# Channel mixers of a two-layer encoder: a tile's convolution tap and its adding transfer stand behind the next tile's weight sums and weights' adding transfer

## The chip, the cores and the metric

One core of a Trainium2 chip runs the whole program in one launch. The metric is the device time of that launch in microseconds (us). Engines are named as in the profile: PE (matrix products), DVE (VectorE), ACT (ScalarE), POOL (GpSimd) and SP (SyncE); SP and POOL also issue DMA transfers.

## What is computed

The program is a trunk of two layers over 512 tokens of width 1024: a layer with an RWKV-7 time mixer, and one with chunked attention; each also attends to 256 memory tokens, and each ends in a channel mixer. Only the channel mixers matter here:

```python
def conv_glu(h, w_in, conv_w, conv_b, w_out):
    seq = h.shape[1]
    gate, val = jnp.split(h @ w_in, 2, axis=-1)
    gp = jnp.pad(gate, ((0, 0), (CONV_W - 1, 0), (0, 0)))
    conv = conv_b + sum(conv_w[j] * gp[:, j:j + seq] for j in range(CONV_W))
    return (jax.nn.gelu(conv, approximate=False) * val) @ w_out

# in each layer
x = x + conv_glu(rms_norm(x, ln2[layer]), ffn_in[layer], ffn_conv[layer],
                 ffn_conv_b[layer], ffn_out[layer])
```

All is float32. The hidden width is 2816, which is 22 tiles of 128 channels; the convolution has three taps along the tokens.

## The kernel before

Every float32 product is made of three products of a faster type: an operand is split into a high part (ACT casts it) and a low part (what the cast left, by a subtraction on DVE or by a transfer that adds), and high x high, high x low and low x high are summed in PSUM.

`ffn` computes a channel mixer with the hidden channels on the partitions and the 512 tokens along the free dimension. Tiles 0 to 20 of the 22 are objects of the class `Seven`: instead of eight half-size products a tile takes seven, by sums and differences of blocks (a Strassen-like scheme). For that each tile needs sums of its weight blocks. A tile's raw weights lie in a buffer `raw` of seven 128x512 blocks: G1, V1, G2, V2 are loaded (`load`, on SP's queue, two tiles ahead), and the rest are sums:

- `sums` (L515) makes S3 and S1 in one operation on DVE, `sum2` (L520) makes S2 from S1, `sum4` (L524) makes S4 from S2.
- `rest` (L499, L500) makes the low part of G2 and V2: ACT writes the negated high part into `wlv`, and a transfer on POOL's queue adds the raw weights from DRAM to it.
- `high` (L528) casts two blocks on ACT: G1 with S2, then S3 with S1, then G2 with V2, then S4. `lower` (L533) subtracts on DVE.
- Nine tiles of the 21 (even numbers 2 to 18, `apart`) make the low part of G1 by a transfer too (`rest1`, L505 and L506); for them DVE makes only the low part of S2 (`both`, L510). The others make both in one wider L533. So tiles alternate between two kinds.

The end of a tile runs while the next two are multiplied: `end1` (L539) and `endr` (L542) finish the gate `g` and scale it by the norm, `end2` (L555) starts `c` on ACT with the third tap and the bias, `end3` (L559) adds the second tap on DVE, `endt` (L545) scales the first tap on ACT into a spare block (in r1h, r1l, r2h or r2l), and `endd` (L552) adds that block to `c`, two tokens later, by a transfer on POOL's queue. One tile later `end4` (L562) is the Gelu on ACT and `end5` (L566) the product with the value half, on DVE.

`frame` writes one tile's work out by hand, in this order around the change: the product of the gate weights, the casts of G2 and S4, the low parts of S3 and S4, the `end1`, `endr`, `end2` and `endt` of the tile before (`prev`), the difference L603, then the changed place, then `end4` and `end5` of the tile before that (`prev2`), L616, and the low part of the next tile's G1 and S2. `keep` pins the instructions of ACT and DVE in the order written; each engine runs its own in order. The transfers of POOL's queue are not pinned, but each stands in its queue in order too. L500 and L506 fill weights of the next tile (`nxt`); PE uses L500's late in that tile, as L465.

The edited lines run where a tile has one before and one behind it: tiles 1 to 19, in two mixers, 38 times in all.

Of the kernel before, what the change touches and what calls it, by code (L numbers as in the profile page):

```python
# [90 lines left out]
def halved(t):  # L91
    return t.rearrange("p (a b) -> p a b", a=2)


def plain_order(ps):
    return ps.rearrange("p (b a) -> p a b", a=2)
# [37 lines left out]
def trunk_kernel(ctx, tc, A, out):  # L134
# [52 lines left out]
    def ps_f():  # L187
        return banks["F"].tile([P, S], F32, name="psf", tag="psf")
# [8 lines left out]
    def tmp(dt=F32, shape=(P, S)):  # L197
        return banks["tmp"].tile(list(shape), dt, name="tmp", tag="tmp")
# [67 lines left out]
    def run(g):  # L266
        for y in g:
            assert not callable(y) or y()
# [166 lines left out]
    def ffn(l, hp, U, T, new_x, xT, after=None, tokens=None):  # L435
# [10 lines left out]
        def prod(ps, w, x, late=False):  # L446
            (wh, wl), o, *ol = w
            ol = ol[0] if ol else o
            for ks in ((0, 1, 2), (3,)) if late else (range(4),):
                for k in ks:  # L450
                    for n in range(2):
                        PE.matmul(ps, wh[:, o + k * P:o + k * P + P], x[k][n], start=k == n == 0, stop=False)  # L452
                for k in ks:
                    PE.matmul(ps, wl[:, ol + k * P:ol + k * P + P], x[k][0], start=False, stop=k == 3)  # L454

        def high_part(ps, w, x):
            (wh, _), o = w
            for k in range(4):
                for n in range(2):
                    PE.matmul(ps, wh[:, o + k * P:o + k * P + P], x[k][n], start=k == n == 0, stop=False)  # L460

        def low_part(ps, w, x):
            (_, wl), o = w
            for k in range(4):
                PE.matmul(ps, wl[:, o + k * P:o + k * P + P], x[k][0], start=False, stop=k == 3)  # L465
# [3 lines left out]
        def keep(ins):  # L469
            return tc.keep_in_program_order(ins) if pinned[0] else ins  # L470
# [5 lines left out]
        class Seven:  # L476
# [91 lines left out]
            def frame(self, prev2, prev, nxt, norm=None, ending=None):  # L568
                first = prev is None
                if first:  # L570
                    nxt.load()
                f1, f2, f3, self.f4 = (ps_f() for _ in range(4))
                g = self.g = tmp()
                prod(f1[:, h1], (self.gs, 0), XU(0, 0))
                if first:
                    hv = self.hv
                    turns["whi"] = (turns["whi"] + 1) % 3
                    self.h31 = self.high(S3)
                    turns["whi"] = (turns["whi"] + 1) % 3
                else:  # L580
                    hv = self.high(G2)
                keep(SC.copy(halved(g[:, h1]), plain_order(f1[:, h1])))
                if nxt and nxt.apart:
                    nxt.rest1()
                if first:
                    prod(self.f4[:, h1], ((hv, self.lows[0]), 0), XU(1, 0), True)
                if norm and not first:
                    run(norm)
                w31 = self.lower(S3, self.h31)
                if prev:  # L590
                    prev.end1()
                    prev.endr()
                prod(f2[:, h1], (self.gs, S), XT(T2), first)
                w4 = self.lower(S4, self.high(S4, S), S)
                if self.j + 2 < NFF - 1:
                    made[self.j + 2].load()
                if nxt and prev:
                    prev.end2()
                    prev.endt()
                elif prev:  # L600
                    next(ending)
                    next(ending)
                keep(V.tensor_tensor(halved(g[:, h2]), halved(g[:, h1]), plain_order(f2[:, h1]), op=ALU.subtract))  # L603
                if nxt and prev:
                    prev.end3()
                    prev.endd()
                if nxt:
                    nxt.sums()
                    nxt.sum2()
                    nxt.rest()  # L610
                if nxt and prev2:
                    prev2.end4()
                    prev2.end5()
                c = self.c = tmp()
                prod(f1[:, h2], (w31, 0), XT(T3))
                keep(V.tensor_tensor(halved(c[:, h1]), plain_order(f1[:, h2]), halved(g[:, h2]), op=ALU.subtract))  # L616
                if first:
                    next(norm)
                prod(f3[:, h2], (w31, S), XT(T1))
                if nxt:  # L620
                    if nxt.apart:
                        nxt.both()
                    else:
                        nxt.gs = nxt.lower(G1, nxt.high(G1))
                    nxt.sum4()
                else:
                    next(ending)
                if first:
                    next(norm)
                v = self.v = tmp()  # L630
                if first:
                    prod(f3[:, h1], ((hv, self.lows[1]), S, 0), XT(T4))
                else:
                    both = ((f3[:, h1], ((hv, self.low), S), XT(T4)), (self.f4[:, h1], ((hv, self.low), 0), XU(1, 0)))
                    for p in both:
                        high_part(*p)
                    low_part(*both[0])
                keep(V.tensor_tensor(v[:].rearrange("p (h a b) -> p h a b", h=2, a=2), halved(c[:, h1]).unsqueeze(1).to_broadcast([P, 2, 2, P]),  # L638
                                     f3[:].rearrange("p (h b a) -> p h a b", h=2, a=2), op=ALU.add))
                keep(V.tensor_tensor(halved(g[:, h2]), halved(g[:, h2]), plain_order(f3[:, h2]), op=ALU.subtract))  # L640
                if nxt:
                    nxt.h31 = nxt.high(S3)
                else:
                    next(ending)
                if not first:
                    low_part(*both[1])
                prod(self.f4[:, h2], (w4, 0), XU(1, 1))
# [1427 lines left out]
```

## Time and profile before

| | us |
|---|---|
| three runs | 1267.63, 1269.70, 1272.45 |
| their median | 1269.7 |
| the profiled execution | 1270.51 |
| its span, first to last instruction | 1268.7 |
| busy: PE, weight loads (PEld), DVE, ACT, POOL | 1229.1, 1078.4, 1032.1, 839.8, 151.1 |
| the first mixer's tiles | about 392 to 592 |
| the second mixer's tiles | about 940 to 1140 |

The granted clock was 0.996 over the span. A row of the timeline gives start, duration, engine, source line, operation, the names out<-in, the shapes and how often; in brackets stands how long the engine had been idle before and who ended that. In a row of waits stand the total, the number and the longest, in us. "DMA to landing" is the time from issue to the last byte's signal, min, median and max.

### The profile page before, as it was taken

Reading aid. Unit: us, or ns where it says so; the run is one execution under the profiler, and the core shown is the slowest. Engines: PE = TensorE matmul, PEld = TensorE weight load, DVE = VectorE, ACT = ScalarE, POOL = GpSimd, SP = SyncE. Lnnn points to the kernel's source line nnn. Section 1 sums busy time; section 2 is a strip of 40 time slices with the busy share of each in tenths; the row PEclk is TensorE's granted clock in tenths of the full one; section 3 lists DMA queues with packets and bytes.
Section 4 is the critical chain, followed back from the end, with each engine's and each line's share of the span. In section 5 each row is a group of like instructions: output and inputs, shape, how many; then the busy total and the mean of one; then the engine's idle time right before and its main releaser. Section 6 shows DMA issues by size and latency. Waiting matters only on the chain.

```text
span 1268.7 us, 26433 instructions
## 1 busy us (share of the span) xinstructions
PE 1229.1 (97%) x10420; PEld 1078.4 (85%) x10420; DVE 1032.1 (81%) x1958; ACT 839.8 (66%) x1396; POOL 151.1 (12%) x180
## 2 busy tenths in 40 slices
PE   9999999999999999999999999999999999999997
PEld 6787777777788999999888878777789999998886
DVE  7976677766678999999886976658889999999785
ACT  6557668766566777776564676767767777765672
POOL 1000000000001222221120000000002322211200
PEclk9999999999999999999999999999999999999999
DMA  6355454353064989985994332233428989878961
GB/s 207 101 166 125 89 114 90 84 117 101 3 199 101 203 205 201 211 195 135 308 217 144 97 112 67 84 108 133 133 51 192 215 204 202 200 160 258 245 177 67
DMA packets 95293, 191.10 MB, mean 151 GB/s; under 512 B 22080, under 2 KB 30400, under 8 KB 95168
## 3 DMA queue, kind: packets, MB, share of 16 engines
q1 hardware_dynamic: 68592, 129.14, 32.4%
q0 software_dynamic: 26576, 60.26, 26.9%
q8 instruction: 82, 1.34, 0.4%
q14 instruction: 43, 0.35, 0.1%
HBM read 173.15 MB, written 6.29 MB: 141 GB/s over the span
## 4 chain that ended last, share of the span: by engine, by line
PE 47%; DVE 26%; ACT 11%; issue 10%; DMA 6%; SPq 0%; ACTq 0%; POOL 0%; DVEq 0%; POOLq 0%
PE psf L735 7%; PE psd L261 4%; PE psf L740 3%; PE psd L257 3%; PE psd L258 3%; PE psd L735 3%; PE psf L452 3%; ACT whi L528 3%; DVE raw L515 3%; DMA wlv<-in_ffn_in_dram 2%; DVE wlo L215 2%; DVE wlo L533 2%; DVE tmp L539 2%; DVE raw L524 2%; DVE tmp L638 2%
## 5 line engine op out<-in xcount | busy, mean ns | idle before, releaser
L528 ACT CAST whi<-raw 128x1024 fp32r<-128x1024 f32 (+1 forms) x168 | 150.2, 938 | 45.4 <-DVE raw L520 24.6
L207 ACT CAST whi<-wraw 128x1024 fp32r<-128x1024 f32 x84 | 87.3, 1045 | 69.5 <-PE psd L258 33.8
L452 PE MATMUL psf<-th,whi 128*128 128x256 f32 x512 | 122.5, 278 | 2.0 <-ACT whi L528 2.0
L452 PE MATMUL psf<-tl,whi 128*128 128x256 f32 x512 | 122.2, 277 | 0.0
L533 DVE TENSOR_TENSOR wlo<-raw,whi 128x1024 fp32r<-128x1024 f32 (+1 forms) x108 | 109.1, 1011 | 6.3 <-ACT whi L528 6.3
L257 PE MATMUL psd<-r1h,whi 128*128 128x512 f32 x264 | 104.0, 395 | 0.0
L258 PE MATMUL psd<-r1l,whi 128*128 128x512 f32 x264 | 101.6, 386 | 0.0
L452 PEld LDWEIGHTS psf<-th,whi 128*128 128x128 f32 x512 | 98.9, 194 | 2.5 <-ACT whi L528 2.4
L452 PEld LDWEIGHTS psf<-tl,whi 128*128 128x128 f32 x512 | 99.1, 193 | 0.0
L215 DVE TENSOR_TENSOR wlo<-wraw,whi 128x1024 fp32r<-128x1024 f32 x67 | 81.6, 1218 | 20.8 <-ACT whi L207 20.3
L725 ACT CAST whi<-raw 128x1024 fp32r<-128x1024 f32 (+1 forms) x52 | 49.3, 951 | 54.6 <-PE psf L735 27.1
L726 DVE TENSOR_TENSOR wlo<-raw,whi 128x1024 fp32r<-128x1024 f32 (+1 forms) x52 | 56.6, 1097 | 31.1 <-ACT whi L725 29.4
L555 ACT ACTIVATE tmp<-tmp,vec 128x512 f32<-128x512 f32 x44 | 36.1, 820 | 62.7 <-DVE tmp L542 62.7
L454 PE MATMUL psf<-th,wlo 128*128 128x256 f32 x504 | 77.6, 276 | 0.0
L261 PE MATMUL psd<-r1h,wlo 128*128 128x512 f32 x264 | 70.4, 389 | 1.0 <-DVE wlo L215 1.0
L454 PEld LDWEIGHTS psf<-th,wlo 128*128 128x128 f32 x504 | 67.0, 193 | 0.0
L500 POOL DMA_DIRECT2D wlv<-in_ffn_in_dram x40 | 60.0, 1500 | 55.0 <-DVE wlo L533 53.9
L257 PEld LDWEIGHTS psd<-r1h,whi 128*128 128x128 f32 x264 | 49.8, 189 | 9.1 <-issue 2.1
L258 PEld LDWEIGHTS psd<-r1l,whi 128*128 128x128 f32 x264 | 49.9, 189 | 6.4 <-issue 0.7
L261 PEld LDWEIGHTS psd<-r1h,wlo 128*128 128x128 f32 x264 | 47.8, 189 | 8.2 <-DVE wlo L215 1.4
L515 DVE TENSOR_TENSOR raw<-raw 128x1024 f32<-128x1024 f32 x42 | 51.1, 1217 | 0.0
L257 PE MATMUL psd<-r2h,whi 128*128 128x512 f32 x128 | 50.3, 394 | 0.5 <-ACT r2h L1705 0.3
(622 smaller groups left out, 3736.7 us busy)
## 6 DMA issues: line engine op xcount, KB each, us to landing
raw<-in_ffn_in_dram SPq DMA_DIRECT2D x42, 512.0 KB, 4.7
raw<-in_ffn_in_dram SPq DMA_DIRECT2D x84, 256.0 KB, 5.4
wlv<-in_ffn_in_dram POOLq DMA_DIRECT2D x40, 512.0 KB, 8.5
raw<-in_ffn_out_dram SPq DMA_DIRECT2D x30, 512.0 KB, 5.4
raw<-in_ffn_out_dram POOLq DMA_DIRECT2D x24, 512.0 KB, 9.4
wraw<-in_wA_dram SPq DMA_DIRECT2D x20, 512.0 KB, 4.3
wraw<-in_w_out_dram SPq DMA_DIRECT2D x16, 512.0 KB, 4.0
wraw<-in_ffn_outp_dram SPq DMA_DIRECT2D x16, 512.0 KB, 4.5
```

Source lines behind the costliest of these rows:

```text
L207: high = lambda: pin(SC.copy(hi[:, :n], raw))
L215: pin(V.tensor_tensor(lo[:, :n], raw, hi[:, :n], op=ALU.subtract))
L257: PE.matmul(ps, wh[:, j * P:(j + 1) * P], ah, start=start and n == 0, stop=False)
L258: dense_at[0] = PE.matmul(ps, wh[:, j * P:(j + 1) * P], al, start=False, stop=False)
L261: dense_at[0] = PE.matmul(ps, wl[:, j * P:(j + 1) * P], moving(act(k))[0], start=False, stop=stop and n == len(ks) - 1)
L452: PE.matmul(ps, wh[:, o + k * P:o + k * P + P], x[k][n], start=k == n == 0, stop=False)
L454: PE.matmul(ps, wl[:, ol + k * P:ol + k * P + P], x[k][0], start=False, stop=k == 3)
L500: GP.dma_start(self.low[:].rearrange("p (a s) -> p a s", a=2), self.second, accum_op=ALU.add)
L515: keep(V.tensor_tensor(raw[:, S3:S1 + 1], raw[:, G1:V2 + 1:3], raw[:, V1:V1 + 1].to_broadcast([P, 2, S]), op=ALU.add))
L528: keep(SC.copy(hi[:, :n], self.pair(what) if n > S else self.raw[:, what]))
L533: keep(V.tensor_tensor(lo[:, :n], self.pair(what) if n > S else self.raw[:, what], hi[:, :n], op=ALU.subtract))
L735: PE.matmul(ps[:], a[:, k0 + i, ts], woven(hi[:, i * S:i * S + S]), start=bool(first) and (first is True or t in first) and a is act[0] an ...
```

## The change

Two groups of lines in `frame` change places. After it, the next tile's weight sums (`sums`, `sum2`) and its adding transfer (`rest`) stand ahead of the tile before's second tap (`end3`) and its adding transfer (`endd`).

```diff
                 keep(V.tensor_tensor(halved(g[:, h2]), halved(g[:, h1]), plain_order(f2[:, h1]), op=ALU.subtract))
-                if nxt and prev:
-                    prev.end3()
-                    prev.endd()
                 if nxt:
                     nxt.sums()
                     nxt.sum2()
                     nxt.rest()
+                if nxt and prev:
+                    prev.end3()
+                    prev.endd()
                 if nxt and prev2:
                     prev2.end4()
                     prev2.end5()
```

On VectorE, at the end of tile 1's frame and in all that follow (`tmp` is the gate `g` or the convolution `c`, `vec` the taps, `raw` the next tile's weights), these rows change places:

```order
 L533 TENSOR_TENSOR wlo<-raw,whi 128x512
 L603 TENSOR_TENSOR tmp<-tmp,psf 128x256
-L559 SCALAR_TENSOR_TENSOR tmp<-tmp,vec 128x511
-L515 TENSOR_TENSOR raw<-raw 128x1024
-L520 TENSOR_TENSOR raw<-raw 128x512
+L515 TENSOR_TENSOR raw<-raw 128x1024
+L520 TENSOR_TENSOR raw<-raw 128x512
+L559 SCALAR_TENSOR_TENSOR tmp<-tmp,vec 128x511
 L566 TENSOR_TENSOR sp<-tmp 128x512
 L616 TENSOR_TENSOR tmp<-psf,tmp 128x256
```

L559, the second tap, moved behind L515 and L520, the sums; nothing else moved on VectorE.

On GpSimd's queue in the first tiles of the first mixer (`wlv` is the low part of G2 and V2, `wlo` that of G1, `tmp<-r1h` the tap's transfer) stood before:

```order
L500 DMA wlv<-in_ffn_in_dram 128x2x512
L506 DMA wlo<-in_ffn_in_dram 128x512
L552 DMA tmp<-r1h 128x510
L500 DMA wlv<-in_ffn_in_dram 128x2x512
L552 DMA tmp<-r1l 128x510
L500 DMA wlv<-in_ffn_in_dram 128x2x512
L506 DMA wlo<-in_ffn_in_dram 128x512
```

and stands now:

```order
L500 DMA wlv<-in_ffn_in_dram 128x2x512
L506 DMA wlo<-in_ffn_in_dram 128x512
L500 DMA wlv<-in_ffn_in_dram 128x2x512
L552 DMA tmp<-r1h 128x510
L500 DMA wlv<-in_ffn_in_dram 128x2x512
L552 DMA tmp<-r1l 128x510
L506 DMA wlo<-in_ffn_in_dram 128x512
```

Each L552 moved behind the L500 that had followed it. The rows of PE and ScalarE are the same before and after.

## The prediction

> **What bounds the kernel now.** I read the page's busy line first, then the busy times of a steady stretch of a channel mixer, then the waits of the engines in it, then the timeline of two neighbouring tiles, engine by engine, and last the landings of GpSimd's transfers.
>
> The busy time of each engine over a steady stretch of the first mixer (its length, then busy us of PE, PEld, DVE, ACT and POOL, then granted clock, DMA share and GB/s):
>
> ```profile
> 425.55:580.00 154.45, 152.87 (x1343) 150.96 (x1342) 148.81 (x225) 112.31 (x151) 40.30 (x39) 1.00 0.90 203
> ```
>
> PE is busy in nearly all of it, but VectorE (DVE) too, and the DMA engines are at 0.90. So nothing here has much room, and the order of the work decides. The timeline of VectorE over one tile, and where the next two begin (L515 is the start of a tile's weight sums):
>
> ```profile
> 463.18 0.41 DVE L603 TENSOR_TENSOR tmp<-tmp,psf 128x256 f32<-128x256 f32 x1
> 463.56 0.75 DVE L559 SCALAR_TENSOR_TENSOR tmp<-tmp,vec 128x511 f32<-128x511 f32 x1
> 464.22 1.22 DVE L515 TENSOR_TENSOR raw<-raw 128x1024 f32<-128x1024 f32 x1
> 465.48 0.69 DVE L520 TENSOR_TENSOR raw<-raw 128x512 f32<-128x512 f32 x1
> 466.09 0.68 DVE L566 TENSOR_TENSOR sp<-tmp 128x512 f32<-128x512 f32 x1
> 466.69 0.42 DVE L616 TENSOR_TENSOR tmp<-psf,tmp 128x256 f32<-128x256 f32 x1
> 467.36 0.69 DVE L510 TENSOR_TENSOR wlo<-raw,whi 128x512 fp32r<-128x512 f32 x1 [0.26 <-ACT whi L528]
> ...
> 473.60 1.22 DVE L515 TENSOR_TENSOR raw<-raw 128x1024 f32<-128x1024 f32 x1
> ...
> 476.06 0.42 DVE L616 TENSOR_TENSOR tmp<-psf,tmp 128x256 f32<-128x256 f32 x1
> 476.79 1.23 DVE L533 TENSOR_TENSOR wlo<-raw,whi 128x1024 fp32r<-128x1024 f32 x1 [0.31 <-ACT whi L528]
> ...
> 483.56 1.22 DVE L515 TENSOR_TENSOR raw<-raw 128x1024 f32<-128x1024 f32 x1
> ```
>
> A tile takes 473.60 - 464.22 = 9.38 us and the next 483.56 - 473.60 = 9.96, a pair 19.34. In each, VectorE stands still exactly once, after L616, for ScalarE's cast of the next tile's gate weights (L528). The waits of VectorE and then of ScalarE in the stretch from 410 to 600 us say the same for the whole mixer (us in total, times, longest):
>
> ```profile
> DVE wlo L533 <- ACT whi L528: 2.8, 9, 0.3
> DVE wlo L510 <- ACT whi L528: 2.0, 8, 0.3
> ```
> ```profile
> ACT whi L528 <- DVE raw L520: 11.2, 16, 0.7
> ```
>
> ScalarE in its turn waits for L520, the second weight sum. Its timeline:
>
> ```profile
> 464.04 1.06 ACT L499 ACTIVATE wlv<-raw 128x1024 fp32r<-128x1024 f32 x1
> 465.00 0.61 ACT L562 ACTIVATE tmp<-tmp 128x512 f32<-128x512 f32 x1
> 466.28 2.94 ACT L528 CAST whi<-raw 128x1024 fp32r<-128x1024 f32 x3 [0.67 <-DVE raw L520]
> ...
> 474.36 0.62 ACT L562 ACTIVATE tmp<-tmp 128x512 f32<-128x512 f32 x1
> 475.70 2.94 ACT L528 CAST whi<-raw 128x1024 fp32r<-128x1024 f32 x3 [0.73 <-DVE raw L520]
> ```
>
> So the loop that sets the time is L559, L515, L520 on VectorE, then the first of the three casts on ScalarE, then L510 or L533 on VectorE again. ScalarE is ready 0.67 us before its operand is.
>
> **The change part by part.** (1) *The tap L559 goes behind the sums.* Its spacing to the next row is 464.22 - 463.56 = 0.66 us, so L515 and L520 start 0.66 earlier and the cast may start at 466.28 - 0.66 = 465.62. Just then ScalarE comes free: Gelu (L562) ends at 465.00 + 0.61 = 465.61. The chain of waits has 1.06 us from 466.28 for the first of the three casts:
>
> ```profile
> 466.28 1.06 ACT whi L528
> ```
>
> It then ends at 466.68. VectorE still does L559, L566 and L616 in the same time as before, so L616 starts at 466.69 as now, and the row behind a 256-wide operation starts 463.56 - 463.18 = 0.38 later, at 467.07. The cast is done 0.39 us before that. The hole closes: L510 moves from 467.36 to 467.07, a gain of 0.29; in the other tile L533 moves from 476.79 to 476.06 + 0.38 = 476.44, a gain of 0.35. VectorE gains 0.64 us in a pair. The edit acts where there is a tile before and one behind, tiles 1 to 19 in each of two mixers: 38 tiles, 19 pairs, 19 x 0.64 = 12.2 us.
>
> (2) *What is late next: PE.* Its timeline (start of a product, start of the next):
>
> ```profile
> 468.82 0.28 PE L452 MATMUL psf<-th,whi 128*128 128x256 f32 x1
> ...
> 470.16 0.28 PE L452 MATMUL psf<-th,whi 128*128 128x256 f32 x1
> ...
> 474.63 0.61 PE L465 MATMUL psf<-th,wlv 128*128 128x256 f32 x4
> ...
> 477.69 0.28 PE L452 MATMUL psf<-r2l,whi 128*128 128x256 f32 x1
> 478.07 0.71 PE L454 MATMUL psf<-r2h,wlo 128*128 128x256 f32 x4
> ```
>
> A product of twelve matmuls takes 470.16 - 468.82 = 1.34 us when nothing is late. Seven make 9.38 a tile, 18.76 a pair, 0.58 below today's 19.34. The last two rows are such a stall: L454 wants the low weights that L533 finishes at 476.79 + 1.23 = 478.02. So PE caps the gain at 19 x 0.58 = 11.0 us. The busy row would leave less (first rival); the page says itself that a busy PE is not PE at its peak. The Trainium skill ("Trainium Kernel Development and Optimization", Performance Expectations) calls matmul busy time a bad measure and weight-load busy time a good one. By its measure, the 150.96 of PEld over 16 tiles, the floor would be 9.43 a tile and the cap 19 x 0.47 = 8.9 us.
>
> (3) *GpSimd's queue: the weights' transfer (L500) goes ahead of the tap's (L552).* Its timeline now:
>
> ```profile
> 464.87 0.86 POOL L552 DMA_DIRECT2D tmp<-r1h  x1 [2.99 <-ACT r1h L545]
> 465.41 1.55 POOL L500 DMA_DIRECT2D wlv<-in_ffn_in_dram  x1
> ...
> 474.85 1.55 POOL L500 DMA_DIRECT2D wlv<-in_ffn_in_dram  x1
> ```
>
> L500 can't be issued much sooner, since ScalarE's L499 ends at 464.04 + 1.06 = 465.10; I cost its issue at nothing. But in its queue the tap's 255 KB no longer stand ahead of it, so it lands sooner. The tap is issued when L559 is done, about 465.48 + 0.61 (L520's spacing) + 0.75 = 466.8, and when L500's 1.55 us of issuing are over, 466.96: some 2.1 us later than now, behind 512 KB. Nothing of the next tiles on GpSimd waits for it; Gelu of the same tile does, on ScalarE, one tile later, and behind Gelu the cast of part 1. From issue to landing, all L552, then the one issued at 464.87; all L500, then those issued at 465.41, 474.85, 484.75 and 504.09:
>
> ```profile
> DMA to landing us min/median/max: 3.6/5.8/8.2
> DMA to landing us min/median/max: 6.0/6.0/6.0
> ```
> ```profile
> DMA to landing us min/median/max: 7.0/8.5/10.2
> DMA to landing us min/median/max: 8.6/8.6/8.6
> DMA to landing us min/median/max: 8.0/8.0/8.0
> DMA to landing us min/median/max: 9.1/9.1/9.1
> DMA to landing us min/median/max: 10.2/10.2/10.2
> ```
>
> The DMA engines in the window 463 to 484, tenths busy in 40 slices:
>
> ```profile
> DMA  9998599999999999983108999999999999759898
> ```
>
> They are full from 465.6 to 472.4, while both transfers run. The same bytes in the other order end at the same time, so I let the tap land when L500 lands now: 8.0 to 10.2 us after L500's issue. Its limit: Gelu starts 474.36 - 465.41 = 8.95 after that issue, a tile becomes 0.29 shorter, and Gelu may slip by the 0.39 of part 1 before VectorE notices: 9.05. For the other tile, with Gelu in this row
>
> ```profile
> 484.34 0.61 ACT L562 ACTIVATE tmp<-tmp 128x512 f32<-128x512 f32 x1
> ```
>
> it is 484.34 - 474.85 - 0.35 + 0.39 = 9.53. So 8.0 is in time with 1.5 to spare, 8.6 in time, 9.1 at the limit, 10.2 late by 1.1. How often? PE wants the landed weights 474.63 - 465.41 = 9.22 after the issue, and waits for them in this many of 40 tiles (us, times):
>
> ```profile
> DMA wlv<-in_ffn_in_dram: 4.1, 10
> ```
>
> Ten landings, then, lie beyond 9.22, and by 0.41 on average: 0.2 to 0.6 beyond the limit of 9.05. Ten times 0.2 to 0.6 is 2 to 6 us; I take 4. These 4.1 us of PE's own waits go, since L500 comes first, but VectorE's period hides them now and I count nothing for them. Below, the loss can be nothing, if the tap lands a little sooner; above, it has no bound but the rival's.
>
> The Trainium skill ("DMA: Bandwidth & Descriptors", Anatomy of one DMA) fits a transfer of GpSimd as 2.0 us plus its bytes over 436 GB/s. That would be 2.6 us for the tap and 3.2 for the weights, where these rows have 6.0 and 8.6; the measurement decides, and by the page's figures no tap would be late and the sum would be PE's cap of 11.0.
>
> (4) *The sum.* VectorE's 12.2 less 4 for late taps is 8.2, under PE's cap of 11.0, so VectorE still sets the period, and 8.2 us is the forecast. The profiled execution took 1270.5 us, 1.8 of it outside its span, and becomes 1262.3. It lies 0.8 above the median of the three runs, 1269.7, which becomes 1261.5. A measurement of this kernel can tell some 0.5%, 6.3 us, from no change: faster is below 1263.4.
>
> **The rivals.** *PE is the bound already.* By its busy time, 152.87 of 154.45 us, only 1.58 us are left in 16 tiles, 0.1 a tile, 3.8 us in 38: 1265.9, the same. For it speaks that row; against it that its waits hide in the modelled ends, as the late L454 shows, and that the period moves with VectorE's hole (9.38 and 9.96 differ by the 512 wider L533, not by PE's work, which is seven products in both). Chance 0.09.
>
> *The taps eat the gain.* If the late landings cost 0.3 to 1.0 us in a pair instead of 0.2, the gain is 6 us or less, or a little below nothing: at 0.64, 1269.7. For it speaks the DMA row, 9 almost throughout, which leaves nothing to make up a delay; against it the odd tiles' 1.5 us of room. Chance 0.14.
>
> *The tap's landing becomes the bound, and it is slower.* Here L500 lands no sooner for going first, since its own 512 KB and the loads beside it set its time, and the tap comes after it. L500 lands 474.0 now, 3.1 after the tap's 470.9; half the bytes would add 1.55. The three landings of such tiles, 8.6, 9.1 and 10.2, mean 9.3; with 1.55 they are 10.85, 1.8 over the limit, and the pair loses 1.8 - 0.64 = 1.16: 19 x 1.16 = 22, 1291.7. It decides from a mean landing of 9.05 + 0.64 = 9.7 on. Against it: full DMA engines move the waiting transfer up when another leaves. Chance 0.12.
>
> *No tap is late at all.* Then PE's cap holds: 1269.7 - 11.0 = 1258.7. For it speaks that 7.0 to 8.6 covers half of the landings. Chance 0.15. That the edit doesn't take effect I leave out: VectorE's and ScalarE's order is pinned, and GpSimd's rows above show the exchange.
>
> **How the numbers follow.** The forecast has 0.50: 1261.5, and with a loss of 2 to 6 us 1259.5 to 1263.5. Together with the fourth rival that is 0.65 faster, the first two 0.23 the same, the third 0.12 slower. The range runs from 1257.5 (VectorE's whole 12.2) to 1270 (the second rival at its even point), and leaves out the slower rival and a part of the second.
>
> **What would show it.** Right: L528's wait for L520 is gone, L510 and L533 follow L616 after 0.38, a pair of tiles takes 18.8 to 19.0, L500 lands 1 to 2 us sooner after its issue and L552 is issued near 467 and lands near 474. Wrong: a pair of 19.3 or more, Gelu (L562) waiting for a tap in most tiles, L566 or L510 idle behind it, or L454 and L452 contiguous while the period stays.

## The result and the profile after

| | before | after |
|---|---|---|
| median of six runs, us | 1270.57 | 1260.13 |
| lowest to highest | 1266.09 to 1272.45 | 1258.14 to 1264.08 |
| span of the profiled execution | 1268.7 | 1258.7 |

The ratio is 0.9929, with a 95% interval of 0.9914 to 0.9944: faster by some 9 us, 7 to 11. The predicted 1261.5 us was 1.4 above the median measured.

Where the time came from is read off L603, which each tile runs once; here are the first and the last of 21 in both mixers. Before:

```profile
394.03 0.41 DVE L603 TENSOR_TENSOR tmp<-tmp,psf 128x256 f32<-128x256 f32 x1
...
593.05 0.41 DVE L603 TENSOR_TENSOR tmp<-tmp,psf 128x256 f32<-128x256 f32 x1
...
942.32 0.41 DVE L603 TENSOR_TENSOR tmp<-tmp,psf 128x256 f32<-128x256 f32 x1
...
1140.91 0.41 DVE L603 TENSOR_TENSOR tmp<-tmp,psf 128x256 f32<-128x256 f32 x1
```

After:

```profile
391.95 0.42 DVE L603 TENSOR_TENSOR tmp<-tmp,psf 128x256 f32<-128x256 f32 x1
...
586.99 0.41 DVE L603 TENSOR_TENSOR tmp<-tmp,psf 128x256 f32<-128x256 f32 x1
...
936.68 0.42 DVE L603 TENSOR_TENSOR tmp<-tmp,psf 128x256 f32<-128x256 f32 x1
...
1130.81 0.42 DVE L603 TENSOR_TENSOR tmp<-tmp,psf 128x256 f32<-128x256 f32 x1
```

The mixers took 199.02 and 198.59 us and take 195.04 and 194.13: 8.4 us less. The two profiled executions differ by 10.0 us: 2.1 more are saved ahead of the first mixer, where the program is the same, and 0.5 are lost again between and behind the mixers. Other executions below reach their first L603 between 389.8 and 394.7, whatever the kernel. Below, "the mixers" is the sum of the two stretches: 397.6 before, 389.2 after. The first tiles of a mixer also vary from one profile to the next, so a second measure leaves them out: "the 18 pairs" are the tiles from the third to the last L515 of both mixers, 349.3 us before and 341.7 after.

VectorE's timeline after, with the two places that are compared (the second, from 470.79 on, is a tile of the other kind):

```profile
459.62 0.41 DVE L603 TENSOR_TENSOR tmp<-tmp,psf 128x256 f32<-128x256 f32 x1
459.95 1.22 DVE L515 TENSOR_TENSOR raw<-raw 128x1024 f32<-128x1024 f32 x1
461.20 0.69 DVE L520 TENSOR_TENSOR raw<-raw 128x512 f32<-128x512 f32 x1
461.81 0.74 DVE L559 SCALAR_TENSOR_TENSOR tmp<-tmp,vec 128x511 f32<-128x511 f32 x1
462.48 0.68 DVE L566 TENSOR_TENSOR sp<-tmp 128x512 f32<-128x512 f32 x1
463.08 0.42 DVE L616 TENSOR_TENSOR tmp<-psf,tmp 128x256 f32<-128x256 f32 x1
463.41 0.68 DVE L510 TENSOR_TENSOR wlo<-raw,whi 128x512 fp32r<-128x512 f32 x1
...
468.93 1.22 DVE L515 TENSOR_TENSOR raw<-raw 128x1024 f32<-128x1024 f32 x1
...
470.79 0.75 DVE L559 SCALAR_TENSOR_TENSOR tmp<-tmp,vec 128x511 f32<-128x511 f32 x1
472.04 0.69 DVE L566 TENSOR_TENSOR sp<-tmp 128x512 f32<-128x512 f32 x1 [0.50 <-ACT tmp L562]
...
479.04 1.22 DVE L515 TENSOR_TENSOR raw<-raw 128x1024 f32<-128x1024 f32 x1
```

The hole behind L616 is gone: L510 follows it after 0.33 us instead of 0.67. The tile from 459.95 takes 8.98 us instead of 9.38. The next should take 9.96 less as much, but VectorE now stands 0.50 us before L566, for Gelu, and it takes 10.11. ScalarE says why, and so do the landings of the two transfers (of the L500 issued at 461.83, and of the L552 issued at 462.85, for which this Gelu waits):

```profile
471.37 0.63 ACT L562 ACTIVATE tmp<-tmp 128x512 f32<-128x512 f32 x1 [0.87 <-DMA tmp<-r1h]
```
```profile
461.83 1.20 POOL L500 DMA_DIRECT2D wlv<-in_ffn_in_dram  x1 [3.85 <-ACT wlv L499]
462.85 1.12 POOL L552 DMA_DIRECT2D tmp<-r1h  x1
```
```profile
DMA to landing us min/median/max: 8.2/8.2/8.2
DMA to landing us min/median/max: 8.5/8.5/8.5
```

The tap was issued 1.02 us behind the weights and landed at 471.35, 1.3 behind them. Gelu began in the same instant, 0.87 us after ScalarE had become free for it. Over the whole execution, the landings of all L500, then of all L552, and the waits for them, by ScalarE and by PE (us, times):

```profile
DMA to landing us min/median/max: 6.0/7.8/9.0
DMA to landing us min/median/max: 6.5/7.9/9.2
```
```profile
ACT tmp L562: 10.2, 14
```
```profile
DMA wlv<-in_ffn_in_dram: 0.2, 1
```

The weights land at a median of 7.8 us instead of 8.5, the taps at 7.9 instead of 5.8. PE hardly waits for weights any more (4.1 us before), and Gelu waits for a tap in 14 of 38 tiles. VectorE in turn stands still before L566, which reads Gelu's result, for 6.8 us in all; these are the rows of the changed kernel (`sp`, r1l and so on are the places that L566 writes):

```profile
DVE sp L566 <- ACT tmp L562: 3.7, 6, 0.9
DVE r1l L566 <- ACT tmp L562: 1.4, 2, 1.2
DVE r2l L566 <- ACT tmp L562: 1.3, 2, 0.9
DVE r2h L566 <- ACT tmp L562: 0.4, 1, 0.4
```

In the kernel before it was 1.8 us.

### The profile page after: what moved, and what is told of

Its sections match the earlier page's. It is cut to its first block, busy times and chain, and to the rows that moved or that the text cites. A ratio compares the mean times of both kernels' runs of the same rounds, so it can differ in the third digit from the quotient of the medians.

```text
span 1258.7 us, 26447 instructions
## 1 busy us (share of the span) xinstructions
PE 1220.2 (97%) x10420; PEld 1074.6 (85%) x10420; DVE 1028.8 (82%) x1958; ACT 841.8 (67%) x1396; POOL 150.9 (12%) x180
## 4 chain that ended last, share of the span: by engine, by line
PE 61%; DVE 15%; ACT 9%; DMA 8%; issue 5%; POOL 1%; SPq 0%; DVEq 0%; ACTq 0%; POOLq 0%
PE psf L452 10%; PE psf L735 7%; PE psf L454 5%; PE psf L460 4%; PE psd L261 4%; PE psf L740 3%; PE psd L735 3%; PE psd L257 3%; PE psd L258 3%; DVE wlo L215 2%; DMA tmp<-r1h 2%; PE psf L465 2%; PE psd L740 2%; PE pss L1855 1%; ACT whi L207 1%
## 5 line engine op out<-in xcount | busy, mean ns | idle before, releaser
L528 ACT CAST whi<-raw 128x1024 fp32r<-128x1024 f32 (+1 forms) x168 | 150.7, 937 | 22.8 <-PE psf L452 17.4
L533 DVE TENSOR_TENSOR wlo<-raw,whi 128x1024 fp32r<-128x1024 f32 (+1 forms) x108 | 109.2, 1013 | 2.0 <-ACT whi L528 1.9
L500 POOL DMA_DIRECT2D wlv<-in_ffn_in_dram x40 | 48.2, 1204 | 250.9 <-ACT wlv L499 193.1
L555 ACT ACTIVATE tmp<-tmp,vec 128x512 f32<-128x512 f32 x44 | 35.9, 816 | 51.0 <-DVE tmp L542 51.0
L515 DVE TENSOR_TENSOR raw<-raw 128x1024 f32<-128x1024 f32 x42 | 51.3, 1220 | 0.0
```

Source lines behind the costliest of these rows:

```text
L528: keep(SC.copy(hi[:, :n], self.pair(what) if n > S else self.raw[:, what]))
L533: keep(V.tensor_tensor(lo[:, :n], self.pair(what) if n > S else self.raw[:, what], hi[:, :n], op=ALU.subtract))
```

## The experiments

Theory H, the prediction's: VectorE's loop through the weight sums, the cast and L510 or L533 sets the period, the closed hole is the gain, and late taps take part of it back. Rival Q: the gain is the weights' transfer going first in GpSimd's queue, so that PE no longer waits for it. Ratios are to the kernel before, run on the same chip.

**1. VectorE's order alone.** `endd` and `rest` are pinned as well, with `endd` first:

```diff
                 if nxt:
                     nxt.sums()
                     nxt.sum2()
-                    nxt.rest()
                 if nxt and prev:
                     prev.end3()
                     prev.endd()
+                if nxt: nxt.rest()
```

> VectorE's order as after the change (L515 and L520 ahead of L559), GpSimd's queue as before (each L552 ahead of its L500). Theory H (the hole on VectorE behind L616 sets the period, and closing it is the gain): the waits of L510 and L533 for L528 are gone, no tap is late, but L500 now queues behind an L552 that waits for the later L559, some 1.9 us later than before, so PE's wait of L465 for the weights grows from 4.1 us to 8 to 20; the time is 1258 to 1267, ratio 0.991 to 0.998. Rival Q (the gain is the weights' transfer going first in the queue): no gain without it, ratio 1.000 to 1.004.

1258.81 us, ratio 0.9928 (0.9914 to 0.9943): the whole gain. The landings of L552 fall to a median of 4.3, those of L500 are 8.1, and PE's wait for the weights is smaller than I expected, 3.0 us instead of 8 to 20:

```profile
DMA wlv<-in_ffn_in_dram: 3.0, 7
```

The mixers took 387.0, the 18 pairs 337.6. In the middle of the first mixer the tiles begin at (with the one wait of VectorE in between)

```profile
481.04 1.22 DVE L515 TENSOR_TENSOR raw<-raw 128x1024 f32<-128x1024 f32 x1
...
489.35 0.69 DVE L533 TENSOR_TENSOR wlo<-raw,whi 128x512 fp32r<-128x512 f32 x1 [0.18 <-ACT whi L528]
...
490.29 1.22 DVE L515 TENSOR_TENSOR raw<-raw 128x1024 f32<-128x1024 f32 x1
...
499.80 1.22 DVE L515 TENSOR_TENSOR raw<-raw 128x1024 f32<-128x1024 f32 x1
```

9.25 and 9.51, a pair of 18.76 us: to the hundredth the cap that the prediction had worked out for PE. The wait that is left stands ahead of the other L533, the low part of S4, whose cast itself waits for PE; and from 520 to 560 us the chain of work that ended last runs through PE's matmuls alone. Before PE binds, the second pair of each mixer took 18.49.

**2. The queue's order alone.** VectorE as before; both transfers pinned:

```diff
-                if nxt and prev:
-                    prev.end3()
-                    prev.endd()
+                if nxt and prev: prev.end3()
                 if nxt:
                     nxt.sums()
                     nxt.sum2()
                     nxt.rest()
+                if nxt and prev:
+                    prev.endd()
```

> VectorE's order as before (L559 ahead of L515 and L520), GpSimd's queue as after (each L500 ahead of the L552 that stood before it). Theory H: the holes of 0.26 and 0.31 us stay, PE's wait of L465 for the weights goes, and the time does not change: ratio 0.998 to 1.003. Rival Q: most of the gain is here, ratio 0.992 to 0.995.

1269.41 us, ratio 1.001 (1.000 to 1.002): nothing. L500 lands at a median of 7.6 and PE's wait for it is gone altogether, but VectorE's waits stay as they were (6.3 and 5.8 before):

```profile
DVE wlo L533 <- ACT whi L528: 6.0, 20, 0.3
DVE wlo L510 <- ACT whi L528: 5.8, 18, 0.9
```

The 18 pairs took 349.3, as in the kernel before. Q has fallen. PE's waits were real, but it had room for them.

**3. Without the tap's transfer** (the first tap is left out of tiles 1 to 19):

```diff
                 if nxt and prev:
                     prev.end3()
-                    prev.endd()
```

> The changed kernel without L552, so the first tap of the convolution is left out in tiles 1 to 19 (the scaled gate is still made by L545). Theory H with late taps as its loss: Gelu (L562) never waits for a transfer, the 6.9 us that VectorE stands still before L566 go, a pair of tiles takes 18.6 to 18.8 instead of 18.5 to 20.3, and the time is 1253 to 1257 (ratio 0.986 to 0.990). If the late taps are hidden behind PE: as the changed kernel, 1259 to 1262 (0.992 to 0.994).

1256.69 us, ratio 0.9907 (0.9888 to 0.9926), the mixers 385.3. VectorE's waits before L566 fell from 6.8 us to 1.9, and the kernel before has 1.8, at the mixers' ends:

```profile
DVE sp L566 <- ACT tmp L562: 1.9, 2, 0.9
```

So late taps cost the changed kernel about 389.2 - 385.3 = 3.9 us in the mixers, and 341.7 - 335.8 = 5.9 in the 18 pairs. The DMA engines also have less to do here, so some of that may not be the late taps'. Over whole runs the two ratios' intervals overlap (0.9888 to 0.9926 and 0.9914 to 0.9944).

**4. Gelu later, nothing left out.** L528's first cast ahead of Gelu, L566 behind L510 or L533, L524 in its place:

```diff
...
                 if nxt:
-                    nxt.sums()
-                    nxt.sum2()
+                    nxt.sums(); nxt.sum2()
                     nxt.rest()
+                    hi1 = nxt.high(G1)
...
                 if nxt and prev2:
                     prev2.end4()
-                    prev2.end5()
+                if nxt: nxt.sum4()
...
                     if nxt.apart:
-                        nxt.both()
+                        nxt.both(hi1)
                     else:
-                        nxt.gs = nxt.lower(G1, nxt.high(G1))
-                    nxt.sum4()
+                        nxt.gs = nxt.lower(G1, hi1)
+                    if prev2: prev2.end5()
```

> The changed kernel with Gelu (L562) behind the first of the three casts, its product L566 behind L510 or L533, and L524 ahead of L616 in its place, so that a tap may land 1.1 us later at no cost; nothing is left out. Theory H with late taps as its loss: the same as without the tap, 1253 to 1257 (ratio 0.986 to 0.990), VectorE's waits before L566 gone. If the late taps are hidden behind PE, or the longer way of L566 costs as much: 1259 to 1262 (0.992 to 0.994).

1258.35 us, ratio 0.9920 (0.9907 to 0.9934), between the two expectations. Gelu waits for a tap in two tiles only (1.2 us), but L566 now stands straight ahead of L638, which needs the buffer that L566 has read:

```profile
501.69 0.68 DVE L566 TENSOR_TENSOR r1l<-tmp 128x512 f32<-128x512 f32 x1
502.47 0.69 DVE L638 TENSOR_TENSOR tmp<-tmp,psf 128x512 f32<-128x512 f32 x1
```

0.78 us from one to the next, where an independent operation of this size follows after 0.60. That is 0.36 in a pair, and 18.49 + 0.36 = 18.85; the pairs take 18.88.

**5 and 6. The changed kernel and the first experiment again, side by side.**

> The changed kernel once more, beside the next run on the same chip. If its late taps cost anything that a whole run shows (the two mixers took 389.2 us here, 385.3 without the tap, 387.0 with the queue's old order), it is 1 to 4 us slower than the next run; if not, the two are the same within 1 us.

> VectorE's new order with GpSimd's old order, as in the first experiment: 0.991 to 0.994 of the kernel before. Theory H: at least as fast as the changed kernel, since the new order of the queue gains nothing; rival Q: slower than it by 2 us or more.

1260.63 us, ratio 0.9938 (0.9924 to 0.9951), and 1258.62 us, ratio 0.9920 (0.9906 to 0.9933). The old order of the queue is the better one by 2.0 us of median, and each of its four runs (1257.22 to 1258.95) is below each of the five of the changed kernel (1258.99 to 1262.28), though the intervals of the ratios overlap. The profiles say the same: the mixers took 389.7 and 386.4. The 18 pairs took 343.1 and 337.3, and 341.7 and 337.6 in the first profiles of the two kernels, so there the exchange in the queue costs 4 to 6 us; in the mixers' other tiles 2 to 3 of them come back, and why is open. The first measurements, on two chips, show no difference (0.9929 and 0.9928). The exchange gains nothing; that it costs 2 to 3 us of the whole time is likely and not settled.

**7. The tap between the two sums** (both transfers pinned in the old order):

```diff
-                if nxt and prev:
-                    prev.end3()
-                    prev.endd()
-                if nxt:
-                    nxt.sums()
-                    nxt.sum2()
-                    nxt.rest()
+                if nxt: nxt.sums()
+                if nxt and prev:
+                    prev.end3()
+                    prev.endd()
+                if nxt:
+                    nxt.sum2()
+                    nxt.rest()
```

> The kernel before with L559 between L515 and L520, GpSimd's queue pinned in the old order: the tap is later, but L520 ends when it did. Theory H, in its sharp form (the cast waits for L520, so only what stands ahead of L520 counts): no change, ratio 0.999 to 1.001, the holes of L510 and L533 stay near 0.3 us. If the gain were in the tap standing later, or in L515 standing sooner: 0.993 to 0.997.

1263.51 us, ratio 0.9959 (0.9944 to 0.9974): my expectation failed, and the time alone lies in the other one's range. VectorE's timeline:

```profile
467.95 0.41 DVE L603 TENSOR_TENSOR tmp<-tmp,psf 128x256 f32<-128x256 f32 x1
468.28 1.22 DVE L515 TENSOR_TENSOR raw<-raw 128x1024 f32<-128x1024 f32 x1
469.41 0.74 DVE L559 SCALAR_TENSOR_TENSOR tmp<-tmp,vec 128x511 f32<-128x511 f32 x1
470.07 0.68 DVE L520 TENSOR_TENSOR raw<-raw 128x512 f32<-128x512 f32 x1
470.68 0.68 DVE L566 TENSOR_TENSOR sp<-tmp 128x512 f32<-128x512 f32 x1
471.28 0.42 DVE L616 TENSOR_TENSOR tmp<-psf,tmp 128x256 f32<-128x256 f32 x1
472.01 1.23 DVE L533 TENSOR_TENSOR wlo<-raw,whi 128x1024 fp32r<-128x1024 f32 x1 [0.31 <-ACT whi L528]
```

The hole of 0.31 stays, as expected: the cast still waits for L520. But L520 itself comes sooner. From L603 to L520 it is 470.07 - 467.95 = 2.12 us where it was 465.48 - 463.18 = 2.30 before. Most of this comes from L515: L520 reads its result and came 1.26 after its start, while L559, which doesn't, starts 1.13 after it, before its 1.22 us are over. The rest comes from L559, which adds to what L555 on ScalarE has written. In the kernel before, L555 ended at 462.70 + 0.82 = 463.52, and L559 started at 463.56, 0.38 behind L603:

```profile
462.70 0.82 ACT L555 ACTIVATE tmp<-tmp,vec 128x512 f32<-128x512 f32 x1 [1.51 <-DVE tmp L542]
```

An operation that has nothing to wait for, L515 here, starts 0.33 behind L603. So the pairs take 19.00 us instead of 19.34, 0.17 less in a tile, hole and all. 38 times 0.17 is 6.5 us; 5.2 were measured by the ratio.

**8. Less work for PE, in the kernel before** (the product of the low weights of G2 is left out of tiles 1 to 20, and the matmul ahead of it ends the sum):

```diff
...
-                if not first:
-                    low_part(*both[1])
```

> The kernel before without the four matmuls of L465 that multiply the low weights of G2 (in tiles 1 to 20; that part of the product is left out): 0.45 us less of PE's work in a tile. Theory H (VectorE's loop sets the period of the kernel before, and PE has room): a pair of tiles still takes 19.33 us, ratio 0.999 to 1.001. Rival (PE is the bound already): 40 times 0.45 us less, 1251 us, ratio 0.986.

1266.72 us, ratio 0.9989 (0.9977 to 1.0000). The tiles begin at

```profile
463.42 1.22 DVE L515 TENSOR_TENSOR raw<-raw 128x1024 f32<-128x1024 f32 x1
472.80 1.22 DVE L515 TENSOR_TENSOR raw<-raw 128x1024 f32<-128x1024 f32 x1
482.76 1.22 DVE L515 TENSOR_TENSOR raw<-raw 128x1024 f32<-128x1024 f32 x1
```

9.38 and 9.96, as with all the matmuls, and 349.2 in the 18 pairs. The rival that PE was the bound already has fallen, for all its 97% of busy time.

**9. Less work for PE, in the first experiment's kernel** (the edits of 1 and 8).

> VectorE's new order with GpSimd's old order, without the four matmuls of L465 that multiply the low weights of G2 in tiles 1 to 20 (that part of the product is left out). If PE caps the gain, as the pairs of 18.76 us in the later half of both mixers of the same kernel with all its matmuls say: all pairs of tiles now take 18.49 us, the two mixers 383 to 384 us instead of 386.4 to 387.0, the time 2 to 4 us less, ratio 0.988 to 0.991. If something else holds the pairs at 18.76: no change, 0.991 to 0.993.

1254.43 us, ratio 0.9888 (0.9869 to 0.9907), the mixers 381.5:

```profile
476.49 1.22 DVE L515 TENSOR_TENSOR raw<-raw 128x1024 f32<-128x1024 f32 x1
485.47 1.22 DVE L515 TENSOR_TENSOR raw<-raw 128x1024 f32<-128x1024 f32 x1
494.98 1.22 DVE L515 TENSOR_TENSOR raw<-raw 128x1024 f32<-128x1024 f32 x1
```

8.98 and 9.51, 18.49 a pair, and so for all pairs from the second on. The mixers are 2 us faster than I expected. The same matmuls that were worth nothing in the kernel before are worth 4 to 5 us here by the ratios, and 3 in the 18 pairs (334.3 against 337.6 and 337.3): with the hole closed, PE is the next bound.

**10. The sums earlier still** (the first experiment with L515 ahead of the low part of S4, to part L520 from L515):

```diff
+                if nxt: nxt.sums()
                 w4 = self.lower(S4, self.high(S4, S), S)
...
-                if nxt:
-                    nxt.sums()
-                    nxt.sum2()
+                if nxt: nxt.sum2()
```

> VectorE's new order with GpSimd's old order, and L515 moved on ahead of the low part of S4 (L533 128x512), so that L520 no longer follows the operation that it depends on; nothing is left out. VectorE's own period falls by about 0.13 us a tile, to 18.2 us a pair. Theory: PE's 18.76 caps it, so the mixers take 385 to 386 us and the time is that of the first experiment or at most 1.5 us less, ratio 0.990 to 0.992. If VectorE were still the bound: 38 times 0.13 us less, 5 us, ratio 0.987 to 0.989.

1263.46 us, ratio 0.9958 (0.9943 to 0.9974): slower than the first experiment, against both expectations. VectorE waits for something new, the load of the raw weights:

```profile
DVE raw L515 <- DMA raw<-in_ffn_in_dram: 11.7, 14, 1.5
```

L515 reads them 0.6 us sooner, and in 14 tiles they have not landed. PE also waits longer for the weights of L500, 11.4 us in 18 tiles where it was 3.0 in 7. A move that gains nothing where PE is the bound has opened a wait on the transfers.

## Why the prediction was right, point by point

*What bounds the kernel* stands. Experiments 2 and 8 took away PE's waits and PE's work without a gain, and 1 closed the hole alone and had all of it.

*VectorE's gain* was taken too small: 0.64 us a pair, by a spacing of 0.38 behind a 256-wide operation. That spacing was read from L603 to L559, and L559 waited there for ScalarE's L555 (experiment 7), not for the 256-wide L603. Behind L616 the spacing is 0.33, and behind L603, where L515 now stands, it is 0.33 too. A tile of one kind went from 9.38 to 8.98, of the other from 9.96 to 9.51 where no tap is late: 0.85 a pair, 16 us over 19 pairs. The Trainium skill ("VectorE: DVE Perf Modes", The DRAIN you can't avoid) says that a semaphore after each operation cost nothing in its chain of copies. Here a wait for the operation ahead does cost: L520, which waits for L515, starts 0.03 us after its end (in the kernel before, 464.22 + 1.22 against 465.48 with rounding), and an independent operation starts some 0.08 before its predecessor's end. For these operations the measurement decides.

*PE's cap* of 18.76 us a pair was right, as experiments 1 and 9 show. PE's busy row would have left 1.58 us in 16 tiles, and the floor from weight-load time, 9.43 a tile, was above the 9.38 that were reached; the product's spacing read from the timeline was the better measure.

*The queue* was right in what counts: no gain from L500's place, and the tap late in some tiles. The detail failed that L500 would land 1 to 2 us sooner after its issue and the tap where L500 had landed. L500 gained 0.7 us at the median, and a tap that Gelu waits for lands about 1.3 after its L500. So 14 tiles were late, not 10, and VectorE lost 6.8 - 1.9 = 4.9 us before L566, against 3.9 in the mixers and 5.9 in the 18 pairs. The forecast had 4. It was also L566, which reads Gelu's result, that stood still, where the prediction's limit of 9.05 had reckoned with L510 and L533, which wait for the cast behind Gelu.

*The sum* of 8.2 us stands against 8.4 in the mixers, 7.6 in the 18 pairs and 9 (7 to 11) in the runs; the second profile of the changed kernel (experiment 5) has 7.9 and 6.2. Part of that is luck: VectorE's gain was 16 and not 12.2 us, but PE's cap and the late taps then took more of it. With late taps VectorE was thought to stay below the cap; in truth cap and taps both bind, at different tiles.

*The slower rival* did not come: it needed a mean landing of 9.7 us after L500's issue in every second tile. The twenty taps of these tiles (from r1h and r2h) landed at a mean of 9.1 after it, by the two transfers' times of issue and landing, and in experiment 5 at 9.3. In the tile shown it was 9.5, and Gelu waited 0.87.

## What to carry to other kernels

When PE, VectorE and the DMA engines are all 90% busy or more, find the one engine whose idle time comes once in each round of a loop, and move out of that loop whatever it doesn't need; busy shares don't tell which engine it is, but taking work from the suspect does (experiments 8 and 9). Work the next bound out before the edit, from the spacing of its instructions: it caps the gain. A transfer that was moved behind another came too late in 14 of 38 tiles here, so look at who needs it; and leave a queue's order alone where it gains nothing.

## What the runs showed of the hardware

The spacing of two VectorE operations depends on whether the second waits for the first. For 512 elements of float32 it was 0.60 us without a wait, 0.71 from L539 to L542, which reads L539's result, and 0.78 from L566 to L638 in experiment 4, which needs the buffer; behind 1024 elements it was 1.13 against 1.26. Placing L559 between L515 and L520, of which the second needs the first, was worth some 0.12 of the 0.17 us a tile in experiment 7.

A GpSimd transfer behind another on the same queue landed after it in all 38 tiles, close behind (1.3 us for 255 KB behind 512 KB in the tile shown, issued 1.02 us later). The Trainium skill ("DMA: Bandwidth & Descriptors", Two DMAs through the same engine are not ordered) says that within one queue a DMA engine starts descriptors in order but pipelines them. These landings agree with that order. In front of the larger one the same transfer lands at a median of 4.3 us (experiment 1; 5.8 in the kernel before), and the larger one then at 8.1 (8.5), not much later than the 7.8 that it took when it stood first.
